# Operand addresses in a two-layer decoder trunk: tiles moved by 128 to 256 bytes, and four identity transposes replaced by one product done in two halves

## The chip, the cores and the metric

The kernel runs on one core of one Trainium2 chip. The metric is the device time of one execution in microseconds (us); of several runs the median is given. A matmul on this core is two instructions: TensorE first loads a stationary operand (128 columns, called the weights below) and then streams a moving operand of up to 512 columns past it. Both operands come from SBUF, the result goes to PSUM.

## The reference

One sequence of 256 tokens, width 1024, goes through two layers. Each layer is: half-step feed-forward network, mixer, second half-step feed-forward network, per-layer embedding gate, each followed by a residual layer norm. The mixer of layer 0 is a forgetting attention with 16 heads of 64, that of layer 1 a latent attention with 16 heads.

```python
def swiglu(x, w_in, w_out):
    h = x @ w_in
    gate, up = h[..., :D_FF], h[..., D_FF:]
    return (jax.nn.silu(gate) * up) @ w_out

for i in range(DEPTH):                                  # DEPTH = 2, D_FF = 2816
    if i == N_A:                                        # N_A = 1
        k_nope, k_rope, v_shared = shared_kv(x, ...)
    x = post_norm(x, 0.5 * swiglu(x, ffn1_w_in[i], ffn1_w_out[i]), ...)
    mix = fox_mixer(x, ...) if i < N_A else mla_mixer(x, ..., k_nope, k_rope, v_shared, ...)
    x = post_norm(x, mix, ...)
    x = post_norm(x, 0.5 * swiglu(x, ffn2_w_in[i], ffn2_w_out[i]), ...)
    gate = jax.nn.sigmoid(x @ ple_w_gate[i] + ple_b_gate[i])
    x = post_norm(x, gate * (p[i] @ ple_w_proj[i]), ...)
```

## The kernel before

**Products.** Every float32 operand is split into a high part (rounded to the type the matmul takes) and a low part (the rest). `mm3` makes one exact product of three matmuls: high by high, high by low, low by high. ScalarE writes the high part (L252, L260), VectorE subtracts it to get the low part (L253, L264). There are 7068 matmuls in the program, nearly all issued through two helpers: `mm` (L616) and `transpose` (L620, a matmul against an identity).

**Weights of the model.** Each weight block comes by DMA into one of three `raw` buffers of 128 x 2048 floats and is split into a slot: ten tiles `hl0` to `hl9` of 128 x 2112 floats, and for some stretches the tiles `gb`, `qk`, `fs`, `ota` and `otb`, which are lent out as further slots and at other times hold attention operands or the combined forms of the feed-forward. `place` cuts the 2048 floats out of a slot's 2112 at an offset `c` (before: 48 floats for the keys that `moves` names, else 0). A `class Stream` with a small model of the engines' times decides when the next block is split; a list `FOX` and a list `ORDER` set the order of steps in the two mixers.

**Feed-forward.** There are eleven chunks of 256 columns. In the three later networks, chunks 0 and 1 are made with the input as stationary operand and the model's weight moving (512 columns, `H`, keys `win`). All the others are made with the model's weight stationary and the transposed input `xT` moving (256 columns, `HT`, keys `wiu`). Groups of chunks are then multiplied with the second weight matrix by a scheme with seven products (`sums`): there the combined form of a chunk, which lies in `fs`, `qk`, `ota` or `otb`, is stationary and the model's weight moves (512 columns). The last three chunks go through plain products (`W`). At the start of a chunk, after six matmuls, `HT` calls `what`: in the later networks a piece of work that is due (transposes of a chunk, of a norm's result), in the first network, where nothing is due, `spare`, four transposes of the identity into a PSUM bank that is overwritten next and whose result nobody reads. In the first network this happens twice, each time in the first chunk after a `sums`.

**Addresses.** Tiles of the pool lie behind one another in the order in which they are first asked for, so a tile's address depends on the sizes of all before it. Within a partition a slot of 2112 floats has 8448 bytes, 33 times 256. For a pair of operands this text gives the remainder of their addresses by 256 bytes, as the built program has them. Before: the ten slots, `gb`, `qk`, `fs`, `g4` (the plain chunks and the values of attention) and `P` have 224; `xT` has 160; `ota` and `otb`, behind a `qk` of 8576 bytes, have 96; a slot shifted by 48 floats has 224 + 192, that is 160. An operand inside a tile begins a multiple of 256 bytes further, if nothing else is said. Where the moving operand and the stationary one have the same remainder they are called *level* below.

Of the kernel before, what the change touches and what calls it, by code (L numbers as in the profile page):

```python
# [10 lines left out]
F32 = mybir.dt.float32  # L11
# [133 lines left out]
class Stream:  # L145
# [74 lines left out]

    def place(self, key, slot):
        w = self.pool.tile([128, 2112], F32R, tag=slot, name=slot, bufs=1)
        c = 48 if moves(key) else 0
        return w[:, c : c + 2048].rearrange("p (i c) -> p i c", i=2)

    def split(self, half=False):
        self.later()
        nc = self.nc
        key = self.order[self.ready]
        g = group_of(key)  # L230
        while self.sums_left(key):
            self.add(g)
        src, parts, n = unit_of(key, self.raw[g], self.sums.get(g))
        if self.aside(key):
            w = self.pool.tile([128, 2, 512], F32R, tag="g4", name="g4", bufs=6)
        else:
            slot = self.slots.pop(0)
            self.slot_of[key] = slot
            w = self.place(key, slot)
        hi, lo = w[:parts, 0, :n], w[:parts, 1, :n]  # L240
        shape = src.shape
        if len(shape) == 3:
            hi = hi.rearrange("p (a b) -> p a b", b=shape[2])
            lo = lo.rearrange("p (a b) -> p a b", b=shape[2])
        elif len(shape) == 4:
            hi = hi.rearrange("p (a b c) -> p a b c", b=shape[2], c=shape[3])
            lo = lo.rearrange("p (a b c) -> p a b c", b=shape[2], c=shape[3])
        t = self.arrives[group_of(key)]
        self.act_t, self.dve_t = max(self.act_t, t), max(self.dve_t, t)

        def both():
            nc.scalar.activation(hi, src, AF.Copy)  # L252
            nc.vector.tensor_tensor(lo, src, hi.bitcast(F32), op=ALU.subtract)  # L253

        if key[0] == "pb":
            nc.gpsimd.memset(w[:, 0, :].bitcast(F32), 0.0)
            lo = w[32:33, 0, :n]
            both()
        elif half:
            nc.scalar.activation(hi, src, AF.Copy)  # L260
            self.busy(act=n)

            def rest():
                nc.vector.tensor_tensor(lo, src, hi.bitcast(F32), op=ALU.subtract)  # L264
                self.busy(dve=n)
                self.split_done(key, w)

            self.rest = rest
            return
        else:  # L270
            both()
        self.pair(n)
        self.split_done(key, w)

    def aside(self, key):
# [148 lines left out]
    return key  # L424


def moves(key):
    return key[0] == "fv" or key[:2] == ("pg", 0)


def unit_of(key, raw, sums=None):

    k, u = key[0], key[-1] % 2
    if k in ("win", "fv"):
        return raw.rearrange("p (k c) -> p k c", c=512)[:, 2 * u : 2 * u + 2, :], 128, 1024
    if k == "wiu":
        return raw[:, 1024 * u : 1024 * u + 1024], 128, 1024
    if k == "ws":
        i = key[-1]
        return ((raw, sums)[i // 2])[:, 1024 * u : 1024 * u + (512 if i == 3 else 1024)], 128, 512 if i == 3 else 1024  # L440
    if k == "fvc":
        n = 816 if key[-1] < 2 else 544
        return raw[:, n * u : n * u + n], 128, n
    if k in ("wout", "fvb", "fo", "pg", "pp", "mo", "qr"):
        return raw[:, 1024 * u : 1024 * u + 1024], 128, 1024
    if k in ("fk", "fq"):
        return raw.rearrange("p (k c) -> p k c", c=256)[:, :, 128 * u : 128 * u + 128], 128, 1024
    if k == "pb":
        return raw[0:1, 0:1024], 1, 1024
    if k == "kd":  # L450
        return raw[:, 640 * u : 640 * u + 640], 128, 640
    if k == "dq":
        return raw[:, 768 * u : 768 * u + 768], 128, 768
    if k == "qn":
        return raw[:, 512:1280], 128, 768
    if k == "kvv":
        return raw[:, 0:1024], 128, 1024
    if k == "kvk":
        return raw[:, 0:512], 128, 512
    raise KeyError(key)  # L460
# [50 lines left out]
class Trunk:  # L511
# [24 lines left out]
    def home(self, homes):  # L536

        if self.rec:
            return None, Dummy()
        self.S.retire()  # L540
        tag = next(t for t in homes if t not in self.S.slot_of.values() and t not in self.taken)
        self.taken.add(tag)
        return tag, self.own([128, 2, 896], F32R, tag)

    def dma(self, out, in_):
# [175 lines left out]
    def ffn(self, li, which, lni, kv=False, ple=False, at=None, cold=False, after=()):  # L721
# [82 lines left out]

            return f

        def HT(c, gate, up, what=None):
            for half in range(2):
                ps = self.bank(*(up if half else gate))
                for u in range(2):  # L810
                    w = self.use(("wiu", li, which, c, 2 * half + u))
                    for kk, b in ((kk, b) for kk in range(4) for b in range(2)):
                        k = 4 * u + kk
                        if (half, k, b) == (0, 1, 0) and what:
                            what(self.bank(*up))
                        col = slice(256 * kk + 128 * b, 256 * kk + 128 * b + 128)
                        self.mm3(
                            ps[:, 256 * b : 256 * b + 256], lambda i: w[:, i, col], lambda i: self.xT[:, :, i, k, :],
                            (k, b) == (0, 0), (k, b) == (7, 1),
                        )  # L820
                if half == 0:
                    gt = self.room(c, summed)
                    nc.scalar.activation(gt, ps, AF.Silu)  # L823
                    S.busy(act=512)
            close(c, gt, ps)
# [123 lines left out]
        else:  # L949
# [14 lines left out]

        turns = (
            None if cold else T(0),
            self.spare if cold else T(1),
            self.kv_transpose if kv else self.ple_transpose if ple else self.spare,
        )
        x = self.turn["h"] if cold else 1 - self.turn["h"]  # L970
        for i, group in enumerate((((1,) + GROUPS[0]) if cold else GROUPS[0],) + GROUPS[1:]):
            for c in group:
                for f in at.get(c, ()):
                    f()
                if c == 2:
                    S.lend("gb")
                if c == 8:
                    S.reclaim("gb")
                if c == 10:
                    S.check("gb")  # L980
                    self.load_gb(li, lni)
                if c == 10 and kv:
                    self.kv_transpose_rope()
                if i == 0 and c == group[0]:
                    banks = ("tr", self.turn["tr"]), ("tr", 1 - self.turn["tr"])
                    turn = turns[0] and (lambda _: turns[0](self.bank("h", 1 - x)))
                    HT(c, *banks, turn)
                else:
                    HT(c, ("h", x), ("h", 1 - x), turns[i] if c == group[0] else None)
            if i < 2:  # L990
                if i == 1 and kv:
                    self.flush()
                sums([c for c in summed if (c < 5 and (cold or c != 1)) == (i == 0)], ("h", x))
                x = 1 - x
            if i == 1:
                S.lend(*after)
                combine()
# [126 lines left out]
    def fox(self, li):  # L1124
# [27 lines left out]
        def VC(t, at={}):  # L1152

            ps = self.bank("y")
            for k in range(8):
                if k in at:
                    at[k]()
                if k % 3 == 0:
                    w = self.use(("fvc", k // 3))
                c = 272 * (k % 3)  # L1160
                self.mm3(
                    ps[:, 0:272], lambda i: self.xT[:, t, i, k, :], lambda i: w[:, i, c : c + 272], k == 0, k == 7)
            if (t, 1) not in v:
                v[t, 1] = self.tl([128, 2, 512], F32R, "g4", 6)
            o = v[t, 1]
            nc.scalar.activation(ftok[:, t, 112:128], ps[:, 256:272], AF.Copy)
            self.parts(o[:, 0, 256:512], o[:, 1, 256:512], ps[:, 0:256])
# [17 lines left out]
        self.tl([128, 8], F32, "gap2", 1)  # L1185
        mb = self.tl([128, 2, 2, 384], F32, "gb", 1)
        cq = self.tl([128, 16, 2], F32, "cq", 1)
        fr = slice(96, 128)
        nc.gpsimd.memset(bf, 0.0)
        if not self.rec:  # L1190
# [284 lines left out]

    def kv_transpose_rope(self):
        nc = self.nc
        self.kr = self.kvt[:, 1088:1856].rearrange("p (i t c) -> p t i c", t=2, i=3)
        kr = [self.kr[:, :, i, :] for i in range(3)]
        b = self.bank("tr")  # L1480
        for t in range(2):
# [20 lines left out]
    def mla(self, li):  # L1502
# [3 lines left out]
            self.dma(qn, pbcast(a["mla_q_norm"][0], QR))  # L1506
        scale = float(192 ** -0.5)
        v = {}
        cqt = self.tl([128, 2, 2, 3, 128], F32R, "gb", 1)
        cqtok = self.tl([128, 2, 768], F32, "PT", 1)  # L1510
        S.reclaim("otb", "qk")
        home = {}
# [422 lines left out]
```

## Time and profile before

| | |
|---|---|
| median of 3 runs | 1049.02 us (1048.88 to 1049.52) |
| profiled execution, its own time | 1049.6 us |
| its span (first to last instruction) | 1047.8 us |
| TensorE busy (PE) | 1035.6 us |
| weight loads (PEld), beside PE | 948.6 us |
| VectorE busy (DVE) | 891.8 us |
| ScalarE busy (ACT) | 592.9 us |
| granted TensorE clock, share of full | 0.998 |

In the profile's rows, `y<-hl,ota` is a matmul from the moving operand `hl` and the stationary operand `ota` into the PSUM tile `y`; `128x512` is 128 partitions by 512 columns of the moving operand; `xT,hl` is `xT` moving and a slot stationary. In the timeline the first column is the start in us from the span's start, the second the length of the merged piece, and `xN` the number of instructions in it. Since a piece's end is modelled and laps over the next one's start, the pace of a run of matmuls is read from start to start: the next piece's start less this one's, by the count.

### The profile page before, as it was taken

What the parts mean: (1) busy time and instruction counts of PE and PEld (TensorE: products, weight loads), DVE (VectorE), ACT (ScalarE), POOL (GpSimd) and SP (SyncE); (2) the same over time, 40 slices, a digit from 0 to 9 for tenths busy, and PEclk for the clock granted to TensorE, in tenths of its full rate; (3) what the DMA queues carried; (4) which work ended last, traced back from release to release, by engine and by line L of the source; (5) the groups of instructions that cost most, each with busy time, mean ns of one, the idle gap of its engine ahead of it and who ended that gap; (6) DMA issues with size and microseconds to landing.
All of it is one profiled execution on the core that took longest, in us unless ns stands there. A gap on an engine that the chain in (4) does not pass through costs nothing.

```text
span 1047.8 us, 17555 instructions
## 1 busy us (share of the span) xinstructions
PE 1035.6 (99%) x7085; PEld 948.6 (91%) x7085; DVE 891.8 (85%) x1312; ACT 592.9 (57%) x901; POOL 58.0 (6%) x88
## 2 busy tenths in 40 slices
PE   9999999999999999999999999999999999999996
PEld 8999898899889999998899898988999889898986
DVE  5788977868898979978979899888887989889877
ACT  6555563666755555663565646646776564646541
POOL 0000000122300000000220000000000000000000
PEclk9999999999999999999999999999999999999999
DMA  7855586455636363673674545743445564555732
GB/s 281 305 191 188 185 298 243 162 168 169 216 128 246 121 252 125 241 282 132 236 260 151 195 169 190 270 142 112 145 156 179 183 214 162 200 190 176 271 125 81
DMA packets 37476, 202.74 MB, mean 193 GB/s; under 512 B 3970, under 2 KB 9874, under 8 KB 16532
## 3 DMA queue, kind: packets, MB, share of 16 engines
q1 hardware_dynamic: 37396, 201.63, 54.3%
q8 instruction: 55, 0.90, 0.3%
q14 instruction: 25, 0.20, 0.1%
HBM read 200.55 MB, written 1.06 MB: 192 GB/s over the span
## 4 chain that ended last, share of the span: by engine, by line
PE 95%; DVE 2%; ACT 1%; issue 1%; DMA 0%; SPq 0%; DVEq 0%; ACTq 0%
PE h L616 53%; PE y L616 29%; PE tr L616 10%; PE tr L620 2%; DVE hl L253 1%; PE h L620 1%; DMA raw<-in_w_dram 0%; PE tr L1375 0%; DVE ts L300 0%; DVE x L705 0%; DVE tr L1720 0%; ACT qk L629 0%; DVE PT L633 0%; DVE ts L306 0%; DVE raw L308 0%
## 5 line engine op out<-in xcount | busy, mean ns | idle before, releaser
L616 PE MATMUL h<-xT,hl 128*128 128x256 f32 x3144 | 366.1, 277 | 1.2 <-ACT hl L327 0.7
L616 PEld LDWEIGHTS h<-xT,hl 128*128 128x128 f32 x3144 | 362.0, 188 | 2.9 <-ACT hl L327 1.2
L253 DVE TENSOR_TENSOR hl<-raw,hl 128x1024 fp32r<-128x1024 f32 (+5 forms) x271 | 314.2, 1190 | 36.1 <-ACT hl L252 35.0
L252 ACT ACTIVATE hl<-raw 128x1024 fp32r<-128x1024 f32 (+5 forms) x271 | 267.8, 1027 | 70.6 <-DVE raw L308 41.3
L616 PE MATMUL y<-hl,g 128*128 128x512 f32 x336 | 78.6, 391 | 0.0
L616 PEld LDWEIGHTS y<-hl,g 128*128 128x128 f32 x336 | 62.5, 188 | 12.6
L616 PE MATMUL h<-hl,xT 128*128 128x512 f32 (+2 forms) x312 | 67.9, 371 | 0.0
L616 PEld LDWEIGHTS h<-hl,xT 128*128 128x128 f32 x312 | 54.9, 188 | 9.8
L616 PE MATMUL y<-hl,otb 128*128 128x512 f32 x219 | 58.0, 399 | 0.0
L264 DVE TENSOR_TENSOR hl<-raw,hl 128x1024 fp32r<-128x1024 f32 (+2 forms) x44 | 52.3, 1192 | 0.8 <-ACT hl L260 0.7
L616 PE MATMUL y<-hl,xT 128*128 128x512 f32 (+3 forms) x282 | 52.7, 334 | 0.0
L260 ACT ACTIVATE hl<-raw 128x1024 fp32r<-128x1024 f32 (+2 forms) x44 | 45.2, 1029 | 9.7 <-DVE raw L308 9.1
L629 ACT ACTIVATE xT<-tr 128x512 fp32r<-128x512 f32 x28 | 16.1, 597 | 58.9 <-PE tr L620 58.9
L616 PEld LDWEIGHTS y<-hl,xT 128*128 128x128 f32 x282 | 44.1, 188 | 4.6 <-ACT xT L629 0.4
L616 PEld LDWEIGHTS y<-hl,otb 128*128 128x128 f32 x219 | 39.8, 188 | 8.4 <-DVE otb L633 0.3
L616 PE MATMUL y<-hl,ota 128*128 128x512 f32 x177 | 46.8, 398 | 0.1
L700 POOL TENSOR_TENSOR rs<-ve,mhalf 128x1 f32<-128x1 f32 x16 | 15.1, 942 | 519.8 <-DVE ve L699 519.8
L616 PE MATMUL tr<-xT,hl 128*128 128x256 f32 x360 | 42.5, 277 | 0.0
L616 PEld LDWEIGHTS tr<-xT,hl 128*128 128x128 f32 x360 | 41.7, 188 | 0.4
L616 PEld LDWEIGHTS y<-hl,ota 128*128 128x128 f32 x177 | 32.7, 189 | 7.7 <-DVE hl L253 0.6
L823 ACT ACTIVATE P<-h 128x512 f32<-128x512 f32 x33 | 19.7, 596 | 33.0 <-PE h L616 32.6
L300 DVE TENSOR_TENSOR ts<-raw 128x1024 f32<-128x1024 f32 x29 | 35.4, 1222 | 0.6
(322 smaller groups left out, 1632.7 us busy)
## 6 DMA issues: line engine op xcount, KB each, us to landing
raw<-in_ffn_in_dram SPq DMA_DIRECT2D x85, 1024.0 KB, 5.0
raw<-in_ffn_out_dram SPq DMA_DIRECT2D x44, 1024.0 KB, 5.0
raw<-in_pg_dram SPq DMA_DIRECT2D x8, 1024.0 KB, 4.9
raw<-in_mo_dram SPq DMA_DIRECT2D x8, 1024.0 KB, 4.8
raw<-in_kq_dram SPq DMA_DIRECT2D x8, 640.0 KB, 4.2
gb<-in_ln_g_dram SPq DMA_DIRECT2D x8, 512.0 KB, 5.9
gb<-in_ln_b_dram SPq DMA_DIRECT2D x8, 512.0 KB, 7.5
raw<-in_fk_dram SPq DMA_DIRECT2D x4, 1024.0 KB, 5.6
```

The costliest lines, as they stand in the source:

```text
L252: nc.scalar.activation(hi, src, AF.Copy)
L253: nc.vector.tensor_tensor(lo, src, hi.bitcast(F32), op=ALU.subtract)
L260: nc.scalar.activation(hi, src, AF.Copy)
L264: nc.vector.tensor_tensor(lo, src, hi.bitcast(F32), op=ALU.subtract)
L300: tt(s[:, 0:1024].rearrange("p (a b) -> p a b", b=512), r[:, 0:512][:, None, :].to_broadcast([128, 2, 512]), r[:, 512:1536].rearrange("p ( ...
L616: self.nc.tensor.matmul(out, lhsT, rhs, start=start, stop=stop)
L620: self.nc.tensor.transpose(out, in_, self.ident)
L629: self.nc.scalar.activation(hi, src, AF.Copy)
L700: nc.gpsimd.tensor_tensor(rs, ve, self.mhalf, op=ALU.pow)
L823: nc.scalar.activation(gt, ps, AF.Silu)
```

## The change

Three tiles without any use (`gap4`, `gap5`, of 32 floats each) and new offsets move operands; no operand's content changes.

- `ota` and `otb` lie 128 bytes further on (96 becomes 224), the tiles behind them 128 or 256.
- `shift` takes the place of `moves`: the keys `win` of the three later networks, `kvv` and `qr` (latent attention) and the gate of layer 0 (`pg`) get 48 floats (224 becomes 160), as `fv` had before; `fvb` and `fvc` get 32 floats.
- `fvc`'s columns, 272 for each of eight rows, are laid at a pitch of 320 floats, so that each begins at remainder 96 (before 224, 32 and 96 in turn); its two splitting instructions write three pieces of 272 in place of 816 in one piece.
- The compressed query `cqt` begins 48 floats into `gb` (224 becomes 160), the rotary key `kr` 32 floats later in `fs` (224 becomes 96).
- The four identity transposes at the two places of the first network go. In their place the seventh product, high by high of `(k, b) = (1, 0)`, is done as two matmuls of 128 columns, one for each half of the tokens, with the same stationary operand. The planner is told the same work as before (`S.busy(pe=1280)`).

In the two built programs, counted over all matmuls with 512 moving columns, 912 of 1899 are level before and 1821 after.

The order of instructions on every engine stays as it is, but for TensorE at these two places and for the shape of the three `fvc` splits. On TensorE at the first place (`h_850` is the bank of the gate half of chunk 5, `hl_823` its weight) before:

```order
L616 MATMUL tr_786<-hl_815,qk 128x512 x3
L616 MATMUL h_850<-xT,hl_823 128x256 x6
L620 MATMUL h_857<-ident 128x128 x4
L616 MATMUL h_850<-xT,hl_823 128x256 x18
L616 MATMUL h_850<-xT,gb 128x256 x24
```

and after:

```order
L622 MATMUL tr_786<-hl_815,qk 128x512 x3
L622 MATMUL h_850<-xT,hl_823 128x256 x6
L828 MATMUL h_850<-xT,hl_823 128x128 x2
L622 MATMUL h_850<-xT,hl_823 128x256 x17
L622 MATMUL h_850<-xT,gb 128x256 x24
```

Four transposes and one matmul of 256 columns have become two of 128. The second place, behind the last three `tr_786<-gb,ota`, changes in the same way.

```diff
     def place(self, key, slot):
         w = self.pool.tile([128, 2112], F32R, tag=slot, name=slot, bufs=1)
-        c = 48 if moves(key) else 0
+        c = shift(key)
         return w[:, c : c + 2048].rearrange("p (i c) -> p i c", i=2)
...
-            hi = hi.rearrange("p (a b) -> p a b", b=shape[2])
-            lo = lo.rearrange("p (a b) -> p a b", b=shape[2])
+            b = n // shape[1]
+            hi = hi.rearrange("p (a b) -> p a b", b=b)[:, :, 0 : shape[2]]
+            lo = lo.rearrange("p (a b) -> p a b", b=b)[:, :, 0 : shape[2]]
...
-def moves(key):
-    return key[0] == "fv" or key[:2] == ("pg", 0)
+def shift(key):
+
+    if key[0] in ("fv", "kvv", "qr") or key[:2] == ("pg", 0) or key[0] == "win" and key[1:3] != (0, "ffn1"):
+        return 48
+    return {"fvb": 32, "fvc": 32}.get(key[0], 0)
...
-        return raw[:, n * u : n * u + n], 128, n
+        return raw[:, n * u : n * u + n].rearrange("p (a b) -> p a b", b=272), 128, n // 272 * 320
...
         self.taken.add(tag)
+        if tag == "ota":
+            self.tl([128, 32], F32, "gap4", 1)
         return tag, self.own([128, 2, 896], F32R, tag)
...
+                        if halve and (half, k, b) == (0, 1, 0):
+                            halve()
+                            o = ps[:, 0:256]
+                            S.busy(pe=1280)
+                            for t in range(2):
+                                nc.tensor.matmul(
+                                    o[:, 128 * t : 128 * t + 128], w[:, 0, col], self.xT[:, t, 0, k, :],
+                                    start=False, stop=False,
+                                )
+                            self.mm(o, w[:, 0, col], self.xT[:, :, 1, k, :], False, False)
+                            self.mm(o, w[:, 1, col], self.xT[:, :, 0, k, :], False, False)
+                            S.pump()
+                            continue
...
             None if cold else T(0),
-            self.spare if cold else T(1),
-            self.kv_transpose if kv else self.ple_transpose if ple else self.spare,
+            None if cold else T(1),
+            self.kv_transpose if kv else self.ple_transpose if ple else None,
         )
+        nothing = lambda: None
+        halve = (None, cold and nothing, cold and nothing)
...
-                c = 272 * (k % 3)
+                c = 320 * (k % 3)
...
+        self.tl([128, 32], F32, "gap5", 1)
...
-        self.kr = self.kvt[:, 1088:1856].rearrange("p (i t c) -> p t i c", t=2, i=3)
+        self.kr = self.kvt[:, 1120:1888].rearrange("p (i t c) -> p t i c", t=2, i=3)
...
-        cqt = self.tl([128, 2, 2, 3, 128], F32R, "gb", 1)
+        cqt = self.tl([128, 1584], F32R, "gb", 1)[:, 48:1584].rearrange("p (t i k c) -> p t i k c", t=2, i=2, k=3)
```

More of the change, by code (lines that the diff above doesn't have):

```diff
@@ L271, in split @@
             both()
-        self.pair(n)
+        self.pair(math.prod(shape[1:]))
         self.split_done(key, w)
@@ L805, in T, with HT @@
             return f
-        def HT(c, gate, up, what=None):
+        def HT(c, gate, up, what=None, halve=None):
             for half in range(2):
@@ L988, in ffn @@
                 else:
-                    HT(c, ("h", x), ("h", 1 - x), turns[i] if c == group[0] else None)
+                    HT(c, ("h", x), ("h", 1 - x), turns[i] if c == group[0] else None, halve[i] if c == group[0] else None)
             if i < 2:
```

## The prediction

> **What bounds the kernel now.** I read the page first: the span, the engines' busy time, then the chain of waits.
>
> ```profile
> span 1047.8 us, 17555 instructions
> PE 1035.6 (99%) x7085; PEld 948.6 (91%) x7085; DVE 891.8 (85%) x1312; ACT 592.9 (57%) x901; POOL 58.0 (6%) x88
> PE 95%; DVE 2%; ACT 1%; issue 1%; DMA 0%; SPq 0%; DVEq 0%; ACTq 0%
> ```
>
> The chain that ended last runs through TensorE for 95% of the span. So nearly every nanosecond between two matmul starts is a nanosecond of the result, and the question is what sets the pace of matmuls that wait for nothing. The page cannot say: its durations are modelled. The timeline of TensorE can, read from start to start. A `sums` stage of the second network:
>
> ```profile
> 361.13 1.52 PE L616 MATMUL y<-hl,qk 128*128 128x512 f32 x6
> ...
> 365.90 1.56 PE L616 MATMUL y<-hl,ota 128*128 128x512 f32 x6
> ...
> 370.78 1.56 PE L616 MATMUL y<-hl,otb 128*128 128x512 f32 x6
> ```
>
> Each form takes 21 matmuls. With `qk` stationary they take 365.90 - 361.13 = 4.77 us, 227.1 ns each; with `ota` 4.88 us, 232.4 ns each. Shape, engine, model weights and bank pattern are the same; what differs is the remainder by 256 bytes (`hl` 224 on `qk` 224, level; on `ota` 96, 128 apart). The second network of layer 0 and the gate behind it give the second pair:
>
> ```profile
> 300.37 2.91 PE L616 MATMUL h<-hl,xT 128*128 128x512 f32 x12
> ...
> 308.62 1.03 PE L620 MATMUL tr<-ident,x 128*128 128x128 f32 x8
> 490.31 1.52 PE L616 MATMUL y<-fs,xT 128*128 128x512 f32 x6
> 491.67 0.62 PE L616 MATMUL y<-hl,xT 128*128 128x512 f32 x2
> ```
>
> Between the first two rows lie 36 matmuls of chunks 0 and 1 with slots at 224 on `xT` at 160: 8.25 us, 229.2 ns each. The gate of layer 0, whose slots are already shifted to 160, runs at 1.36 / 6 = 226.7 ns on the same `xT`. So three paces stand in the trace: level 226.7 ns, 64 apart 229.2, 128 apart 232.4. I take 226.7 for every long level run.
>
> The 256-column matmuls have two paces too, here at the first of the two places that lose their transposes:
>
> ```profile
> 70.92 0.87 PE L616 MATMUL h<-xT,hl 128*128 128x256 f32 x6
> 71.63 0.60 PE L620 MATMUL h<-ident 128*128 128x128 f32 x4
> 71.98 2.30 PE L616 MATMUL h<-xT,hl 128*128 128x256 f32 x18
> 74.12 2.88 PE L616 MATMUL h<-xT,gb 128*128 128x256 f32 x24
> 76.84 27.36 PE L616 MATMUL h<-xT,hl 128*128 128x256 f32 x240
> ```
>
> Before the transposes 0.71 us for 6, 118 ns each; behind them, from 74.12 to 76.84, 113.3 ns each, with the same remainders. [...] So the transposes, useless for the result, are worth 4.7 ns for each matmul behind them, and what replaces them must do that too.
>
> **The change part by part.**
>
> *Combined forms `ota` and `otb`, 96 to 224.* The windows of time, asked for `ota` and then for `otb` alone, give the counts by stage:
>
> ```profile
> 112.00:119.00 7.00, 5.28 (x21) 1.00 0.37 122
> 272.00:300.00 28.00, 12.13 (x48) 1.00 0.48 172
> 364.00:377.00 13.00, 5.04 (x21) 1.00 0.62 221
> 819.00:830.00 11.00, 5.75 (x24) 1.00 0.66 241
> 715.00:819.00 104.00, 10.20 (x48) 1.00 0.42 143
> L620 PE MATMUL tr<-ident,ota x24: 271/272/273, 716.4 to 782.9; 128*128 128x128 f32 x24
> 272.00:300.00 28.00, 12.12 (x47) 1.00 0.48 172
> 715.00:819.00 104.00, 31.21 (x120) 1.00 0.42 143
> ```
>
> A row gives the window, its length, TensorE's busy time and count, then clock and DMA. The first four and the one with x48 at 715 are `ota`, those with x47 and x120 `otb`; 24 of the 48 are transposes. The later networks have six such stretches of 21 + 21, 252 matmuls; at 232.4 - 226.7 = 5.7 ns that is 1.44 us. The output product of the forgetting attention (48 + 47) is partly in long runs, partly in threes and sixes between other work, where the first three or so behind an interruption keep their delay (a six then gains 3 x 5.7, 2.5 to 2.9 ns for each): between that and 5.7 I count 4 ns, 0.38 us. Latent attention has 120 + 24 = 144, nearly all in sixes: 2.5 ns, 0.36 us. The 24 at 819 are one run: 0.14 us. The 21 of the first network stand behind VectorE:
>
> ```profile
> 103.42 2.35 DVE hl L253 x2
> ...
> 114.12 1.42 PE y L616 x5
> ```
>
> These rows of the chain say that from 103.42 to 114.12 VectorE's splits decide when TensorE goes on; only the last dozen gain, 0.07 us. Sum 2.39 us.
>
> *`win`, 224 to 160.* The groups of the window from 299 to 324, one of three such stages:
>
> ```profile
> L616 PE MATMUL h<-hl,xT 128*128 128x512 f32 x72 | 17.4, 393 | 0.0
> L616 PE MATMUL h<-fs,xT 128*128 128x512 f32 x12 | 3.2, 392 | 0.0
> L616 PE MATMUL h<-qk,xT 128*128 128x512 f32 x12 | 3.2, 391 | 0.0
> ```
>
> 96 matmuls, 288 in the three later networks: at 229.2 - 226.7 = 2.5 ns, 0.72 us.
>
> *Other 512-column products* (`kvv`, `qr`, gate and last chunks with `otb` or `ota` moving), some 150 in short runs, together with the transitions into and out of the runs above: between 0 and 0.5 us, taken 0.3.
>
> *`cqt`, 224 to 160, as moving operand of 256 columns.*
>
> ```profile
> 755.53 1.22 PE L616 MATMUL h<-gb,hl 128*128 128x256 f32 x9
> 756.59 0.52 PE L616 MATMUL h<-PT,g 128*128 128x256 f32 x3
> ```
>
> 1.06 us for 9 is 117.8 ns. At 160 the quick pace of 113.3 ns is possible and not certain, as the rows at 70.92 show. Sixteen heads of nine: 0 to 0.65 us, taken 0.3. `fvb`, `fvc` and `kr` move from one unlevel remainder to another: taken as nothing, between -0.1 and +0.1 us, for a hundred or so matmuls that could each differ by 1 ns. The three `fvc` splits write as many elements in another shape; VectorE and ScalarE have no part in the chain there.
>
> *The two places.* Four transposes take 71.98 - 71.63 = 0.35 us, and the 18 behind them 74.12 - 71.98 = 2.14 us in place of 18 x 113.3 = 2.04: 0.45 us for a place. The price of a 128-column matmul with full rows stands in the scores of latent attention:
>
> ```profile
> 758.81 0.43 PE L616 MATMUL tr<-qk 128*128 128x256 f32 x2
> 759.07 0.33 PE L616 MATMUL tr<-fs,xT 128*128 128x256 f32 x1
> 759.24 0.51 PE L616 MATMUL tr<-qk 128*128 128x256 f32 x3
> 759.59 0.40 PE L616 MATMUL tr<-fs,xT 128*128 128x256 f32 x2
> ```
>
> One of 256, one of 128 and one of 256 take 0.43 us, of which some 0.08 to 0.10 are the delay behind transposes (2.14 less 2.04 above); three of 256 take 0.35. So a half product costs about as much as a whole one, 0.115 us, and by its columns at least 0.06. Two of them in place of one add 0 to 0.12 us; with the same settling behind them as behind transposes I take 0.10. A place saves 0.35 us, both 0.70; bounds 0.25 and 0.45 for each. This holds if the halves bring the quick pace. The stretch behind the first place has 18 + 24 + 240 matmuls: without it, 282 x 4.7 = 1.3 us are lost there, and about as much at the second. [...]
>
> *What is late next.* A faster TensorE asks VectorE for slots sooner. The tightest stage is the second `sums` of a later network:
>
> ```profile
> 408.00:427.00 19.00, 19.00 (x90) 15.75 (x89) 18.62 (x23) 10.48 (x13) 0.00 (x0) 1.00 0.39 129
> 715.00:830.00 115.00, 114.47 (x751) 103.27 (x750) 99.31 (x235) 78.30 (x188) 0.92 (x1) 1.00 0.44 153
> ```
>
> Third in a windows row stand TensorE, weight loads, VectorE: 18.62 of 19 us, so VectorE has 0.38 us to give, and TensorE would gain 42 x 5.7 = 0.24 there. It fits, barely, and the next stage gives VectorE room. In the attentions some matmuls wait for a softmax or a split, and what is saved just ahead of such a wait is lost; by the idle 115.00 - 114.47 = 0.53 us in latent attention these waits are few. I take off 0.35 us.
>
> *Sum.* 2.39 + 0.72 + 0.3 + 0.3 + 0.70 - 0.35 = 4.06 us, off the profiled execution's 1049.6. Its runs' median is 1049.02, 0.6 us lower; the same saving gives **1044.9 us**.
>
> [...]
>
> **Rivals.**
>
> 1. *The halves do not bring the quick pace.* For it: not every interruption does. After two transposes here
>
> ```profile
> 210.12 2.99 PE L616 MATMUL h<-xT,hl 128*128 128x256 f32 x24
> 212.95 0.38 PE L620 MATMUL tr<-ident,fs 128*128 128x128 f32 x2
> 213.09 5.08 PE L616 MATMUL h<-xT,hl 128*128 128x256 f32 x41
> ```
>
> the pace was 2.83 / 24 = 118 ns ahead, and it did not change: 41 matmuls took 5.08 us behind two transposes, where the piece of 18 above with 23 more at 113.3 ns would have taken 2.30 + 2.61 = 4.91. Against it: behind four transposes at this very place in the program the pace changed. If both places fail, 2.6 us come back: 1047.5. If one fails, 1046.2.
>
> 2. *The waits move.* VectorE, at 98% of the tight `sums` stages, and the softmaxes take half of what the remainders give: (2.39 + 0.72 + 0.3 + 0.3) / 2 = 1.85 less, 1.5 beyond what I took off: 1046.4. Against it: chain at 95% TensorE.
>
> 3. *Addresses do not matter*, and `ota`'s pace came from what VectorE and ScalarE did meanwhile. Then only the places are left: 1049.02 - 0.70 = 1048.3. Against it: the level and unlevel runs lie side by side under the same VectorE load.
>
> 4. *The other side: the quick pace is lost elsewhere.* The later networks also start their stretches of some 280 narrow matmuls behind a `sums` or `win` run, and a switch by transposes. If entering from level runs, which these become, leaves them slow, each of some eight stretches costs 1.3 us: 1044.9 + 10 = 1055. It is slower than before from the fifth stretch on (4.1 / 1.3 = 3.2, plus the margin). Against it: the first place is entered from level runs already, on `qk`, and switches.
>
> That the change does not do what it says I leave aside: the remainders were read from the built programs.
>
> **How the numbers follow.** My forecast gets 0.74, one place failing 0.06, both 0.08, the second rival 0.06, the third 0.03, the fourth 0.03. The unknown prices are +-0.3 (other products), +-0.3 (`cqt`), +-0.2 (places), +-0.4 (waits), and the attentions' narrow matmuls may fall into either pace, +-0.7; together about +-1.1 round 1044.9. The range reaches up to rivals 1 and 2: 1043.3 to 1047.3. A measurement of this kernel can tell about 0.2%, 2.1 us, from no change, so faster means below 1046.9: forecast, one place failing and most of the second rival, 0.85; same 0.12 (both places failing, the third rival, the rest); slower 0.03.
>
> **What will show it.** In the timeline after: `y<-hl,ota` and `otb` in `sums` at 226.7 ns from start to start, and `h<-hl,xT` too; behind the two halves 113.3 ns, with no more than 0.25 us lost around them; `h<-gb,hl` below 117.8; span near 1043.7 with VectorE's busy time unchanged. It is wrong if those runs keep 232 and 229 ns, if the stretches behind the halves run at 118 ns, or if idle time of TensorE grows in `sums` and the attentions by more than 1 us.

## The result

The changed kernel takes 1045.73 us (median of 6 runs, 1044.22 to 1046.78) against 1049.27 us (median of 6 runs of before, 1048.88 to 1050.36, on the same chip): a ratio of 0.9964, 95% interval 0.9952 to 0.9976, so 3.5 us faster. The forecast was 1044.9. Timed once more later, beside the experiments, the changed kernel had a ratio of 0.9957 (0.9942 to 0.9972). The profiled execution took 1046.14 us. Its page, with the span, the engines' busy time and the chain of waits by engine:

```profile
span 1044.4 us, 17541 instructions
PE 1032.8 (99%) x7079; PEld 949.2 (91%) x7079; DVE 891.9 (85%) x1312; ACT 593.3 (57%) x901; POOL 58.9 (6%) x88
PE 91%; DVE 6%; ACT 1%; issue 1%; DMA 0%; DVEq 0%; SPq 0%; ACTq 0%
```

The span is 3.4 us shorter, TensorE's busy time 2.8 us, VectorE's unchanged. VectorE's share of the chain rose from 2% to 6%; where, is shown below.

The timeline of TensorE in the `sums` stage of the second network, the one that the prediction read:

```profile
360.48 1.52 PE L622 MATMUL y<-hl,qk 128*128 128x512 f32 x6
...
365.24 1.52 PE L622 MATMUL y<-hl,ota 128*128 128x512 f32 x6
...
370.00 1.52 PE L622 MATMUL y<-hl,otb 128*128 128x512 f32 x6
...
374.76 0.87 PE L622 MATMUL h<-xT,hl 128*128 128x256 f32 x6
```

From row to row 4.76 us for 21 matmuls three times over, 226.7 ns each: `ota` and `otb` now run as `qk` does. Chunks 0 and 1 of this network (36 matmuls between the two rows):

```profile
299.88 2.91 PE L622 MATMUL h<-hl,xT 128*128 128x512 f32 x12
...
308.07 1.03 PE L626 MATMUL tr<-ident,x 128*128 128x128 f32 x8
```

8.19 us, 227.5 ns each where it was 229.2. The first of the two places:

```profile
72.51 0.33 PE L828 MATMUL h<-xT,hl 128*128 128x128 f32 x2
72.68 2.15 PE L622 MATMUL h<-xT,hl 128*128 128x256 f32 x17
74.67 2.88 PE L622 MATMUL h<-xT,gb 128*128 128x256 f32 x24
77.39 27.36 PE L622 MATMUL h<-xT,hl 128*128 128x256 f32 x240
```

From 72.51 to 74.67 the eighteen products, one of them as halves, take 2.16 us, 0.12 more than 18 x 113.3 ns; behind them 24 take 2.72 us, 113.3 ns each. The quick pace is there, as behind the transposes, and the place costs 0.12 us in place of 0.45.

In the two profiled executions the saving would have been larger but for the opening, chunks 0 to 4 of the first network, which the change does not touch. The timeline there, first of the kernel before, then of the changed one:

```profile
28.75 27.36 PE L616 MATMUL h<-xT,hl 128*128 128x256 f32 x240
61.38 1.54 PE L616 MATMUL y<-hl,fs 128*128 128x512 f32 x6
```

```profile
28.37 28.43 PE L622 MATMUL h<-xT,hl 128*128 128x256 f32 x240
62.29 1.52 PE L622 MATMUL y<-hl,fs 128*128 128x512 f32 x6
```

In the profile of before these 240 matmuls ran at the quick pace, in that of after at the slow one, and the first `sums` began 0.91 us later. Matched matmul by matmul from start to start, the two profiles differ by +0.89 us up to the first place and by -4.3 us behind it.

Where VectorE now takes part is the second `sums` stage of the second network. The windows of time, as in the prediction, and the timeline at the stage's end:

```profile
408.00:427.00 19.00, 19.00 (x87) 15.75 (x86) 18.61 (x23) 10.48 (x13) 0.00 (x0) 1.00 0.41 148
715.00:830.00 115.00, 114.30 (x755) 103.21 (x754) 99.46 (x235) 80.54 (x192) 0.93 (x1) 1.00 0.44 153
428.26 0.66 PE L626 MATMUL h<-ident,g 128*128 128x128 f32 x4 [0.22 <-DVE x L903]
```

VectorE still has 18.61 of 19 us, and TensorE, earlier by now, waits 0.22 us for it at 428.26; from 388 to 427 the chain that ended last runs largely through VectorE. In latent attention TensorE is idle for 0.70 us in place of 0.53.

### The profile page after: what moved, and what is told of

Same layout as the page of the kernel before. It is cut to its first block, busy times and chain, and to the rows that moved or that the text cites. A ratio compares the mean times of both kernels' runs of the same rounds, so it can differ in the third digit from the quotient of the medians.

```text
span 1044.4 us, 17541 instructions
## 1 busy us (share of the span) xinstructions
PE 1032.8 (99%) x7079; PEld 949.2 (91%) x7079; DVE 891.9 (85%) x1312; ACT 593.3 (57%) x901; POOL 58.9 (6%) x88
## 4 chain that ended last, share of the span: by engine, by line
PE 91%; DVE 6%; ACT 1%; issue 1%; DMA 0%; DVEq 0%; SPq 0%; ACTq 0%
PE h L622 51%; PE y L622 28%; PE tr L622 9%; PE tr L626 2%; DVE hl L254 2%; DVE ts L301 1%; PE h L626 0%; DVE ts L307 0%; DVE raw L309 0%; ACT qk L635 0%; ACT hl L253 0%; DVE g L254 0%; PE tr L1397 0%; DVE P L848 0%; DVE hl L265 0%
```

## The experiments

Expectations are quoted as they were recorded before each run. Kernels whose order of instructions could have moved were given the planner's costs that keep it, so that on every engine the order is that of the kernel they are compared with. "Quick" is 113.3 ns and "slow" about 118 ns for a 256-column matmul, from start to start.

### The parts apart: addresses, halves, neither

The first kernel is the changed one with the transposes left in:

```diff
-            None if cold else T(1),
-            ... self.ple_transpose if ple else None,
+            self.spare if cold else T(1),
+            ... self.ple_transpose if ple else self.spare,
...
-        halve = (None, cold and nothing, cold and nothing)
+        halve = (None, None, None)
```

> The kernel before with every address move of the change, and the four transposes kept at both places. Theory A (the difference of the two operands' remainders by 256 bytes sets the pace of a 512-column matmul, and TensorE passes a saved nanosecond on to the end): 4.06 - 0.70 = 3.4 us below the kernel before, about 1045.7, with up to 1.2 us either way by the pace that the opening of the first network happens to fall into; y<-hl,ota and y<-hl,otb in the sums at 226.7 ns from start to start. [...] Rival (the waits take what the addresses give): half, 1.7 us below, 1047.4.

The second is the kernel before with `HT`'s halves and the `turns` of the change:

```diff
-            self.spare if cold else T(1),
-            ... self.ple_transpose if ple else self.spare,
+            None if cold else T(1),
+            ... self.ple_transpose if ple else None,
...
+        halve = (None, cold and nothing, cold and nothing)
```

> The kernel before with the halves alone: one product done as two of 128 columns in place of four transposes at both places, no address moved. Theory A: 0.35 us at each place, 0.7 us below before, about 1048.4, and 113.3 ns behind both places; the opening's pace can add or hide 1.2 us. Rival (the halves bring the quick pace only where the run ahead of them is level): in this kernel y<-hl,qk ahead of the places is level anyway, so no difference. Rival (the places give nothing): 1049.

The third is the changed kernel with neither; the line stands for the planner's cost alone:

```diff
                         if halve and (half, k, b) == (0, 1, 0):
-                            halve()
-                            ... two of 128 columns, two of 256
-                            continue
+                            S.busy(pe=1014)
```

> The changed kernel with neither transposes nor halves at the two places: the product there is three plain matmuls of 256 columns, all else in the same order on every engine. Theory A: both stretches of some 282 narrow matmuls run at 118 ns as they are entered; 2 x (282 x 4.7 ns - 0.2 us) = 2.2 us above the changed kernel, about 1047.9. Rival (the change of pace comes by itself, or from the stretch's entry behind a level run, and the halves only cost): 0.2 us below the changed kernel, 1045.5.

Measured on one chip, with before at 1049.68 us (26 runs):

| kernel | median (runs) | ratio to before, 95% |
|---|---|---|
| addresses alone | 1046.38 (10) | 0.9969 (0.9960 to 0.9978) |
| halves alone | 1048.26 (11) | 0.9986 (0.9978 to 0.9995) |
| neither halves nor transposes | 1047.42 (11) | 0.9980 (0.9970 to 0.9990) |

The addresses alone give 3.3 us, against 3.4 expected. Of that profile, matched with before, the 512-column matmuls give 3.5 us. It also held a surprise at the first place, where four transposes stand as in the kernel before:

```profile
71.07 0.60 PE L626 MATMUL h<-ident 128*128 128x128 f32 x4
71.42 2.37 PE L622 MATMUL h<-xT,hl 128*128 128x256 f32 x18
73.62 2.99 PE L622 MATMUL h<-xT,gb 128*128 128x256 f32 x24
76.45 28.43 PE L622 MATMUL h<-xT,hl 128*128 128x256 f32 x240
```

From 73.62 to 76.45 24 matmuls take 2.83 us, 117.9 ns: the transposes did not bring the quick pace, and the stretch lost 1.27 us against before. At the second place of the same run they did. So transposes are no sure switch.

The halves alone moved the starts behind the two places by -0.34 and -0.35 us (0.35 each was predicted), while the same profile lost 0.70 us in the opening, which turned slow on the way. The median's 1.4 us is more than 0.7, but its interval (0.5 to 2.3) holds it.

Without either, both stretches stayed slow from entry to end:

```profile
73.97 2.99 PE L622 MATMUL h<-xT,gb 128*128 128x256 f32 x24
76.80 28.43 PE L622 MATMUL h<-xT,hl 128*128 128x256 f32 x240
```

2.83 us for 24, 117.9 ns. Against a profile of the changed kernel with a quick opening, its matmuls fall behind by 1.14 and 1.13 us at the two places; 1.1 each was expected. The medians (1047.42 against 1045.21 and 1045.73 of the changed kernel) give 1.7 to 2.2 us. So in this kernel the pace does not come by itself, and the rival falls. What stands ahead of a stretch matters too: over the eleven profiles that have the slots at 224, a stretch entered from 512-column matmuls at less than 228 ns began slow in all 102 cases, one entered from slower ones began quick, without any interruption, in 5 of 30.

### Is it the pair of addresses?

`ota` and `otb` are put back at 96 by leaving out the change's unused tiles (there are two, `gap4` and `gap5`, not three), and the moving operand of the sums is put at 96 too. From here to the opening each kernel has one profiled run.

```diff
-        if tag == "ota":
-            self.tl([128, 32], F32, "gap4", 1)
...
-        self.tl([128, 32], F32, "gap5", 1)
...
-    return {"fvb": 32, "fvc": 32}.get(key[0], 0)
+    return {"ws": 32, "fvb": 32, "fvc": 32}.get(key[0], 0)
```

> The changed kernel with ota and otb back at remainder 96 and the ws slots (the moving operand of the sums) put at 96 too. Theory A: y<-hl,ota and y<-hl,otb in the sums are level again and take 226.7 ns from start to start, while y<-hl,fs and y<-hl,qk, untouched at 224, are now 128 apart and take 232.4. Rival (the place of ota and otb in SBUF makes them slow, not the pair): ota and otb 232.4, fs and qk 226.7 as in the kernel before. The products outside the sums that read ota and otb are 128 apart again (0.7 us back); the total should be near 1045.7 + 0.7 + 1.4 to 1.9, about 1048.

It took 1050.35 us. The timeline of the same `sums` stage:

```profile
355.50 1.56 PE L620 MATMUL y<-gb,fs 128*128 128x512 f32 x6
...
360.40 1.55 PE L620 MATMUL y<-hl,qk 128*128 128x512 f32 x6
...
365.29 1.55 PE L620 MATMUL y<-hl,ota 128*128 128x512 f32 x6
...
370.11 1.55 PE L620 MATMUL y<-hl,otb 128*128 128x512 f32 x6
...
373.53 0.84 PE L620 MATMUL y<-gb,otb 128*128 128x512 f32 x3
374.21 0.85 PE L620 MATMUL tr<-g,otb 128*128 128x512 f32 x3
```

`fs` takes 4.90 us for 21, 233.3 ns, and `qk` 4.89, 232.9, though neither has moved. `ota` takes 4.82, but its first eight carry a delay over from `qk`; from then on, and in the row at 373.53, it is 226.7 ns. The slow pair has become the quick one and the quick pair slow, with the same tiles in the same roles: what counts is the pair, not where either operand lies. Matched with the changed kernel, the `fs` and `qk` matmuls lost 2.0 us (1.4 to 1.9 expected). The total is 2 us above the expectation since two stretches of 256-column matmuls (at 375 and at 907 us) stayed slow behind four transposes, 1.0 us each.

A 512-column matmul here costs 6 ns more or nothing (232.9 to 233.3 ns against 226.7), by the addresses of the two operands relative to each other; why the pair counts, no run shows.

How does the cost grow with the distance? `ota` at 160, `otb` at 192, slots at 224:

```diff
-            self.tl([128, 32], F32, "gap4", 1)
-        return tag, self.own([128, 2, 896], F32R, tag)
+            self.tl([128, 16], F32, "gap4", 1)
+        o = self.own([128, 2, 896], F32R, tag)
+        if tag == "ota":
+            self.tl([128, 8], F32, "gap6", 1)
+        return tag, o
...
-        self.tl([128, 32], F32, "gap5", 1)
+        self.tl([128, 40], F32, "gap5", 1)
```

> The changed kernel with ota at remainder 160 and otb at 192 instead of 224 for both; slots stay at 224, so the moving operand is 64 bytes ahead of ota and 32 ahead of otb. Theory A (the pace follows the difference of the remainders): y<-hl,ota in the sums at 229.2 ns from start to start, as slots at 224 on xT at 160 took before; y<-hl,otb between 226.7 and 229.2; with 21 of each in a stage and 126 of each in the later networks 0.3 us and 0 to 0.3 us above the changed kernel. Rival (only the 96 and 224 of the stationary matter, or something that comes with the allocation): 226.7 or 232.4 for both.

```profile
363.57 1.52 PE L625 MATMUL y<-hl,qk 128*128 128x512 f32 x6
...
368.33 1.53 PE L625 MATMUL y<-hl,ota 128*128 128x512 f32 x6
...
373.15 1.56 PE L625 MATMUL y<-hl,otb 128*128 128x512 f32 x6
...
378.05 0.87 PE L625 MATMUL h<-xT,hl 128*128 128x256 f32 x6
```

64 apart, `ota`: 4.82 / 21 = 229.5 ns, as expected. 32 apart, `otb`: 4.90 / 21 = 233.3 ns, as slow as 128 apart and not between 226.7 and 229.2. A distance matters, but not in proportion: level is quickest, 64 apart costs 2.5 to 2.8 ns, 32 and 128 cost 6 (the moving operand ahead each time). (The run took 1052.45 us. Matched with the changed kernel's second profile, which appears below, 2.0 us of it are a slow opening, 2.2 in the networks' 256-column stretches, some of them with `ota` and `otb` as slots at new remainders; 1.8 in the 512-column matmuls on `ota` and `otb`.)

### What the 256-column matmuls need

Their stationary operand, the slots of the keys `wiu`, is moved network by network. `xT` stays at 160.

```diff
+    if key[0] == "wiu":
+        return {(0, "ffn1"): 48, (0, "ffn2"): 32, (1, "ffn1"): 16}.get(key[1:3], 0)
```

> The changed kernel with the stationary slots of the 256-column products (wiu) moved, network by network: remainder 160 in the first network (level with the moving xT at 160), 96 in the second (moving 64 ahead), 32 in the third (128 apart), 224 in the fourth as before (moving 64 behind). What is open is why these products run now at 113.3 and now at 118 ns. Theory A1 (the two paces are two states of any such stream, whatever the addresses): both paces in every network. Theory A2 (a remainder decides there too, as with 512 columns): one network at 113.3 ns from its first matmul on, with no stretch at 118, worth up to 4.7 ns for each of some 980 matmuls that run slow now, 4.6 us in the whole kernel; another at 118 throughout, whose 960 matmuls would cost up to 4.5 us. From the kernel before, where cqt was level at 117.8 for most of its 144, level should not be the quick one.

The second such kernel:

```diff
+    if key[0] == "wiu":
+        return {(0, "ffn1"): 8, (0, "ffn2"): 24, (1, "ffn1"): 40, (1, "ffn2"): 56}[key[1:3]]
```

> The changed kernel with the stationary slots of the 256-column products at four more remainders: 0 in the first network (moving xT at 160, so 96 behind the stationary's next 256), 64 in the second (moving 96 ahead), 128 in the third (32 ahead), 192 in the fourth (32 behind). In the run before, level gave 118 ns throughout, 128 apart a jitter of 113 to 123 with a mean near 118.6, and 64 apart either 113.3 or 118 for a whole stretch. Theory A2 (a remainder decides): one of the four at 113.3 ns in all its stretches, opening included; moving every slot there would then be worth up to 4.6 us. Rival (only 64 apart allows the quick pace, as a state that a stretch falls into): no stretch at 113.3 in any of the four, and a time near 1058, some 3000 narrow matmuls x 4.7 ns above the changed kernel.

They took 1057.00 and 1060.78 us; the second was expected near 1058, though the terms given for it (3000 x 4.7 ns) make 1059.8. One piece of 24 matmuls of each network from the timelines; in such a piece the last starts 23 paces behind the first, so 0.11 us more than 2.88 is 4.8 ns for each. First level, then two pieces with `xT` 64 ahead, then 128 apart, then 64 behind as in the kernel before:

```profile
75.63 3.04 PE L624 MATMUL h<-xT,gb 128*128 128x256 f32 x24
...
341.16 2.99 PE L624 MATMUL h<-xT,otb 128*128 128x256 f32 x24
...
410.62 2.88 PE L624 MATMUL h<-xT,hl 128*128 128x256 f32 x24
...
564.64 3.01 PE L624 MATMUL h<-xT,otb 128*128 128x256 f32 x24
...
945.66 2.88 PE L624 MATMUL h<-xT,hl 128*128 128x256 f32 x24
```

And of the second kernel: 96 behind, 96 ahead, 32 ahead, 32 behind:

```profile
74.80 3.01 PE L624 MATMUL h<-xT,gb 128*128 128x256 f32 x24
...
340.42 3.04 PE L624 MATMUL h<-xT,otb 128*128 128x256 f32 x24
...
565.76 2.96 PE L624 MATMUL h<-xT,otb 128*128 128x256 f32 x24
...
947.90 3.00 PE L624 MATMUL h<-xT,hl 128*128 128x256 f32 x24
```

The mean over whole stretches of one network of one run for each distance, settling at the entry left out:

| moving less stationary, bytes | ns from start to start | quick stretches |
|---|---|---|
| 0 | 120.0 | 0 of 2 |
| 32 | 116.7 | 0 of 3 |
| 64 | 113.3 or 117.8 | 1 of 3 |
| 96 | 120.0 | 0 of 3 |
| 128 | 118.7 | 0 of 3 |
| -96 | 118.7 | 0 of 2 |
| -64 (as before and after; 117.8 in those profiles) | 113.3 or 117.8 | 3 of 3 |
| -32 | 118.3 | 0 of 3 |

So the 256-column matmuls want another distance than those of 512: only 64 bytes either way allows the quick pace, and there a stretch has it or lacks it as a whole. Level, the best for 512 columns, is here among the worst, and with it the halves did nothing at either place. No remainder is quick throughout, so theory A2's gain is not to be had, and its rival in the second kernel was right. The kernel's 224 on 160 is as good as any.

### What switches the pace

One identity transpose at the first place, two at the second, no halves:

```diff
                         if halve and (half, k, b) == (0, 1, 0):
-                            halve()
-                            ... two of 128 columns, two of 256
-                            continue
+                            S.busy(pe=1014)
+                            for t in range(halve):
+                                nc.tensor.transpose(..., self.ident, self.ident)
...
-        halve = (None, cold and nothing, cold and nothing)
+        halve = (None, cold and 1, cold and 2)
```

> The changed kernel with one identity transpose at the first place and two at the second, in place of the halves; the product there is three plain matmuls. Rows so far: behind four transposes the quick pace stood in nearly every stretch, behind two transposes that met the slow pace it stayed slow each time, behind two halves it was quick each time, behind nothing slow. Theory A (an interruption switches the pace if it is long or short enough by the columns that TensorE streams behind its loads, so two transposes are as good as two halves): the second place quick, 113.3 ns. Rival (the count of four or the other operands matter, as the rows at 210 us of before say): slow, 118 ns, at both places, and a time 2.4 us above the changed kernel.

It took 1047.29 us. A piece behind each place:

```profile
74.32 2.88 PE L622 MATMUL h<-xT,gb 128*128 128x256 f32 x24
...
147.78 2.99 PE L622 MATMUL h<-xT,ota 128*128 128x256 f32 x24
```

Behind one transpose quick, behind two slow, to the end of the stretch. Neither theory had this. Over the eleven profiles that have the slots at 224 (all but the two of the table above) the stretches count as follows: behind halves quick in 16 of 16 (12 of them met the slow pace), behind four transposes, which all met the slow pace, in 100 of 103, behind one in 1 of 1; behind two that met the slow pace in 0 of 12 (eleven of these are one place of the program), and behind two that met the quick pace it stayed quick in 11 of 11; behind six that met the slow pace in 11 of 13, but of those that met the quick pace only 9 of 20 kept it. One transpose and two halves cost the same, 0.14 and 0.12 us with the settling. Why the number decides stays open.

### The opening, and a version beside the change

A third pair of halves, in chunk 1 of the first network:

```diff
-                            S.busy(pe=1280)
+                            S.busy(pe=1280 if i else 256)
...
-        halve = (None, cold and nothing, cold and nothing)
+        halve = (cold and nothing,) * 3
...
-                    HT(c, *banks, turn)
+                    HT(c, *banks, turn, halve[0])
```

> The changed kernel with a third pair of halves, in chunk 1 of the first network, all else in the same order. In the changed kernel's profile the opening stretch ran at 118 ns, in the profile of before at 113. Theory A: the halves bring 113.3 ns to the rest of the opening, some 425 matmuls x 4.7 ns = 2.0 us less 0.2 for the halves: 1.8 us below a run whose opening is slow, 0.2 above one whose opening is quick by chance; a median of about 1044.3 with a smaller spread than the changed kernel's 2.6 us. Rival (the opening waits for VectorE's splits and the model weights, so that a quicker pace there ends in a wait): no change, 1045.7, idle time of TensorE before the first sums. Rival (the spread comes from somewhere else): spread as before.

Median 1045.49 us (5 runs, 1044.69 to 1046.91), ratio to before 0.9964 (0.9951 to 0.9978): not the 1044.3 expected. So it was run once more on one chip with the changed kernel itself.

> The changed kernel as it is, on the same chip as the kernel with the third pair of halves, so that the two can be compared. Theory A (its opening falls into either pace by chance): 1044.2 to 1047, median near 1045.7, and a profile whose opening is at 113.3 or at 118 ns, the first sums starting about 62.3 us if slow and 60.8 to 61.6 if quick. Rival: the first profile's slow opening is the rule.

> The kernel with the third pair of halves, once more, beside the changed kernel on one chip. Theory A (the halves make the opening quick every time): 0.3 to 1.0 us below the changed kernel in the median, since about half of the changed kernel's openings are slow, 1.8 us each, and the pair costs 0.12; the largest times near 1047 gone. Rival (the opening's length is set by the early waits for data, which run from 0.3 to 1.2 us in the profiles so far, and the spread stays): the same median within 0.3 us and the same spread.

The changed kernel: 1045.21 us (5 runs, 1044.32 to 1047.77). With the third pair: 1044.90 us (5 runs, 1044.36 to 1045.51), ratio to before 0.9951 (0.9937 to 0.9964) against 0.9957 (0.9942 to 0.9972). The intervals overlap nearly wholly, so it cannot be said that it beats the change. This time the changed kernel's opening was quick by itself, so its slow opening was chance (the timeline of this run):

```profile
28.76 27.36 PE L622 MATMUL h<-xT,hl 128*128 128x256 f32 x240
55.96 2.88 PE L622 MATMUL h<-xT,gb 128*128 128x256 f32 x24
```

From row to row 240 matmuls take 27.20 us, 113.3 ns each. Matched with the changed kernel's first profile it is 0.92 us shorter, 0.88 of that in the opening.

Eleven profiles share the opening's operands (all but the two of the table of distances). With a quick opening (six of them) the first `sums` start at 60.8 to 61.6 us; where the pace turns slow on the way, behind a wait (three), at 61.6 to 62.1; where it is slow throughout (two), at 62.3 and 63.4. So the pace is worth what was counted, up to 1.8 us, but it is not the only chance there. The very first matmuls take 213 ns from start to start. The windows of time from 7 to 9 us, of the changed kernel's second profile and of the first with the third pair; TensorE's count is the one in the first bracket:

```profile
7.00:9.00 2.00, 2.00 (x16) 2.00 (x17) 1.46 (x4) 1.51 (x4) 0.00 (x0) 1.00 0.95 299
```

```profile
7.00:9.00 2.00, 2.00 (x11) 2.00 (x11) 0.61 (x2) 0.94 (x3) 0.00 (x0) 1.00 1.04 369
```

16 matmuls against 11, both busy all the time. Of the first matmuls 3 to 23 are at 213 ns in the eleven profiles, 0.1 us lost with each, and waits for the first blocks take 0.3 to 1.7 us. The granted clock in these rows (the column behind the engines) reads 1.00; why the number of such matmuls differs from run to run, no run shows. The profile that missed its expectation had 23 such matmuls, the most of all. So the rival that the spread has another source is right in part. In both profiles with the third pair the opening was quick already ahead of the halves, so what they do there when it is slow was not seen. Whether the smaller spread of the second five runs (1.2 us against 3.5 beside it) is theirs is not settled, since the first five had 2.2.

## Why the prediction was right

The forecast of 1044.9 us was 0.8 us low, the measured time inside the range, and faster was the likeliest. By its steps, matched matmul by matmul between the two profiles:

| term | predicted, us | measured, us |
|---|---|---|
| `ota`, `otb` in the later `sums` (252) | 1.44 | 1.40 |
| the same, forgetting attention (95) | 0.38 | 0.39 |
| the same, latent attention (144) | 0.36 | 0.21 |
| the run of 24, and the first network's 21 | 0.21 | 0.20 |
| `win` (288) | 0.72 | 0.54 |
| other 512-column products, transitions | 0.3 | 0.45 |
| `cqt` (144) | 0.3 | 0.41 |
| the two places | 0.70 | 0.74 |
| waits, and all other matmuls | -0.35 | -0.05 |
| the opening | none | -0.89 |
| sum | 4.06 | 3.40 |

- **Right in mechanism and size:** the three paces of 512-column matmuls, read from one stage of one profile, held in every stage, and the swap shows that the pair of remainders sets them. The halves' price (0.10 predicted, 0.12 measured) and the transposes' (0.45 to 0.46) held, and TensorE's nanoseconds reached the end nearly one for one.
- **Mis-sized:** `win`. I took 229.2 to 226.7 for all 288; in the mean they went from 230.2 to 228.4, since behind an interruption by transposes the first keep an irregular pace after the change too (from 308.86 us of its profile 314, 231, 236, 228, 233 and 231 ns, then 226 to 227; before, from 309.41 us, 318 and then 226 to 232 throughout). Latent attention's sixes and nines, for the same reason, gave 1.5 ns each in place of 2.5.
- **`cqt`:** predicted as possible, not certain, and so it is: the groups behind a quick stretch are quick, others slow. Two groups of nine from the timeline:

```profile
753.64 1.22 PE L622 MATMUL h<-gb,hl 128*128 128x256 f32 x9
...
788.02 1.18 PE L622 MATMUL h<-gb,hl 128*128 128x256 f32 x9
```

Eight paces differ by 0.04 us, 5 ns each; 95 of the 144 matmuls were quick. The table of distances fits: `cqt` was level with its slot, where no stretch was quick, and came to 64 behind it. It does not fit in size, for level `cqt` took 117.8 ns and the long level stretches 120.0.
- **The waits:** named at the right place. VectorE's 0.38 us of room in the tight stage did not suffice (0.22 us of idle time), latent attention lost 0.17. Together 0.39 against 0.35, set off by narrow matmuls that fell the other way.
- **Not in the prediction:** the opening. Its range allowed 0.7 us for the narrow matmuls of the attentions but took the opening as fixed, though the rows of before (the pace that changed behind an interruption) spoke for chance there too. It is the term that the profiled run lost against the sum. (The five unknowns behind the range, their squares added, make 0.93 us and not 1.1; the range was wider than either.)
- **Right in outcome, with no reason shown:** that the halves bring the quick pace, on which the 0.70 us of the two places rest. Behind them 16 of 16 stretches were quick, 12 of which had met the slow pace, but no run shows why. That they are 128 columns wide, as the transposes are, does not explain it: behind two transposes the slow pace stayed in 12 of 12 stretches, and at other distances (level, 120.0 ns, and 96 behind, 118.7) the halves did nothing.

Of the rivals, the first (the halves fail) was met in none of sixteen places. Transposes failed in 3 of 103; whether the halves are the safer of the two, the twelve places where they met the slow pace are too few to tell. The second (the waits take half) falls by the waits measured, 0.39 us where it asked for 1.85. The third (addresses do not matter) falls by the swap. The fourth (the quick pace lost elsewhere) was right in its premise, for behind 512-column matmuls at less than 228 ns every stretch was entered slow, but the interruptions mended it: all nine long stretches of the changed kernel's later networks were quick.

## What to carry to other kernels

When one engine is the whole chain, read its pace from start to start, by form, before anything else: two forms of the same shape at 226.7 and 232.4 ns are worth microseconds, and a few bytes of padding move them. The best distance depends on the shape, so each must be measured (here level for 512 columns, 64 bytes for 256), and a swap of the two operands' places tells the pair from the place. A stream with two paces of its own adds chance to every single profile, so terms should be taken from matched stages and not from spans.

## What the runs showed of the hardware that was not expected

- The cost of a distance between stationary and moving operand is not monotone: for 512 columns 226.7 ns level, 229.5 at 64, 233.3 at 32 and 232.4 to 233.3 at 128 bytes.
- For 256 columns, level takes 120.0 ns (117.8 in the groups of `cqt` before) and 64 bytes either way 113.3 or 117.8, a state that lasts for hundreds of matmuls. An interruption changes the slow one into the quick: four transposes in 100 of 103 stretches, two 128-column products in 12 of 12, one transpose the one time it was tried, two never in 12.
- Behind 512-column matmuls at less than 228 ns such a stretch began slow in 102 of 102 cases, behind slower ones it began quick in 5 of 30.
- Of the first 256-column matmuls of an execution 3 to 23 run at 213 ns in place of 113 to 118, some 1.5 us between the two profiles of the kernel with the third pair (23 against 7), under a granted clock that the profile gives as 1.00.
